# A 32-byte constant that shifts the weight ring of a one-core decoder layer by 32 bytes

## The chip, the core and the metric

The kernel runs on one core of one Trainium2 chip, in one launch. The metric is the time of the device in microseconds (us). Lower is better. Engine names are those of the profile: PE is TensorE (matmuls), PEld its weight loads, DVE is VectorE, ACT is ScalarE, POOL is GpSimd, SP is SyncE, which issues most of the DMAs.

## What is computed

One decoder layer on 512 tokens of width 1024, all in float32. Cut to its frame, the reference is:

```python
h = rms_norm(x, attn_norm[l])
proj = h @ w_in[l]
q_da, k_da, v_da, rw_cols, q_mem = jnp.split(proj, [c1, c2, c3, c4], axis=-1)
o_da = diff_attention(q_da, k_da, v_da, positions, ...)
o_rw = rwkv7_time_mix(rw_cols, ...)
mem_n = rms_norm(mem, mem_norm[l])
o_mem = memory_attention(q_mem, mem_n, w_mem_kv[l], ...)
x = x + jnp.concatenate([o_da, o_rw, o_mem], axis=-1) @ w_out[l]
xn = rms_norm(x, ffn_norm[l])
x = x + hierarchical_moe(xn, w_group_router[l], ..., w_e_gate[l], w_e_up[l], w_e_down[l])
```

The mixture has 16 experts of hidden width 512. Each token goes to two of them. Every expert has three weight matrices of 1024 x 512 numbers, so the expert weights alone are 16 x 3 x 2 MB.

## The kernel before

**The weights.** All weight matrices come through one stream (`WeightStream`, lines 72 to 118). A chunk is 128 partitions x 1024 float32 numbers (512 KB). It is loaded by SP (line 87) into a raw slot, and then split into a high and a low part: ACT rounds it to `whi` (line 96), and DVE subtracts (`wlo`, line 97). Both parts have the type float32r. Raw slots are the ring's `raw0` and `raw1`, later also buffers that are done with (`f`, `kT`, `qT`, `u`, `r_t`, `k_t`, `gg`), the `lraw`, `xhi` and `xlo` tiles of the pool `late`, and five `eraw` tiles of the pool `ex`. The parts sit in four pairs `whi0`/`wlo0` to `whi3`/`wlo3` of the ring, and for a while in two pairs `xhi`/`xlo`. At most 10 loads are in flight.

**The matmuls.** A product is three matmuls (`mm3`, lines 242 to 245): high by high, low by high, high by low. In the trace `pp<-whi,xh` means that `whi` is the moving operand, which streams through the array, and `xh` the stationary one, which the weight load puts there beforehand.

- RWKV columns (`cols_unit`, line 349): the weights are stationary and the normed input `hm_h`, `hm_l` moves, 512 columns a matmul.
- The other projections (`proj`, line 368) and the output projection (`out_part`, line 979): the weights move, 256 columns a matmul, and `hm_h`, `hm_l` (or, for the memory, `v_da`, `qT`) are stationary.
- Experts (lines 1264 to 1347): 96 gathered tokens are stationary (`xh`, `xl`, `hh`, `hl`), and the weights move, 512 columns a matmul. An expert has 48 matmuls for gate and up (`in_product`) and 24 for down (`down`), 8 transposes of the gathered tokens (line 1267) and 4 of the hidden values (line 1289).

**The order.** It is made when the program is built: a weave of generators with priorities, and then a scheduler that simulates the engines. Before the experts stand the projections, woven with the RWKV chain and the attention (to about 285 us), then the second half of the output projection and the routing (to about 342 us), then the experts.

**The places of the buffers.** Each pool takes a stretch of each partition's on-chip memory. On the left, from address 0 upward, lie `const`, `rc`, `wk`, `ring`, `bigr`, and then `biga`, whose place `late` takes over. On the right, up to the end, lie `hm`, later `rt`, then `ex`. Pools take space in steps of 32 bytes. The ring's tiles are 4096 bytes long and follow each other without a gap.

Of the kernel before, what the change touches and what calls it, by code (L numbers as in the profile page):

```python
# [10 lines left out]
F32 = mybir.dt.float32  # L11
# [9 lines left out]
P = 128  # L21
# [7 lines left out]
CAP = 96  # L29
# [40 lines left out]


class WeightStream:
    """Weight chunks in the order of their use: raw load, high part, low part, each in a ring of slots."""

    def __init__(self, tc):
        self.tc, self.nc, self.depth, self.flight = tc, tc.nc, DEPTH, []
# [42 lines left out]


class Weave:
    """Emits the steps of several streams in the order of their estimated times."""

    def __init__(self, tc):
        self.tc, self.live, self.now = tc, [], 0.0
# [25 lines left out]
def hybrid_layer_kernel(ctx, tc, x, mem, positions, cols, w_in, w_kv, w_out, wa2, g2, ffn, wr, br,  # L151
# [4 lines left out]
    const = ctx.enter_context(tc.tile_pool(name="const", bufs=1))  # L156
# [14 lines left out]
    def pp():  # L171
        return psp.tile([P, 512], F32, name="pp", bufs=4)

    def pc():
        return pools["ps"].tile([P, 512], F32, name="pc", bufs=2)

    def pt():
        return pools["ps"].tile([P, 512], F32, name="pt", bufs=2)

    ring = ctx.enter_context(tc.tile_pool(name="ring", bufs=1))  # L180
# [10 lines left out]
    def bR(name, shape, dtype=F32):  # L191
        return bigr.tile(shape, dtype, name=name)

    def b4(name, shape, dtype=F32):
        return biga.tile(shape, dtype, name=name)

# [1 line left out]
    A.preload_act_table_set("sigmoid_and_others")  # L198
    xs = [bR("f1", [P, 2, D]), bR("f2", [P, 2, D])]
    xt = [xs[t // 2][:, t % 2, :] for t in range(NT)]  # L200
# [82 lines left out]
        first = A.activation(hi, ps, AF.Copy, scale=g)  # L283
        return first, V.scalar_tensor_tensor(lo, ps, g, hi.bitcast(F32), op0=ALU.mult, op1=ALU.subtract)

# [1 line left out]
    banks = [pp() for _ in range(4)] + [pt() for _ in range(2)] + [pc() for _ in range(2)]  # L287
    held = [ws.pair.pop() for _ in range(3)]
    ws.pump()
# [35 lines left out]
        V.tensor_scalar(ext[:, E_DQ + h:E_DQ + h + 1], col[:, C_DQ:C_DQ + 1], -0.125 / SLOPES[h], None, op0=ALU.mult)  # L325
    V.tensor_scalar(ext[:, E_SUB:E_SUB + 1], col[:, C_SUB:C_SUB + 1], 1.0 - LAM_INIT, None, op0=ALU.mult)

# [1 line left out]
    r_t = bR("r_t", [P, 2, S])  # L329
    k_t = bR("k_t", [P, 2, S])  # L330
    v_t = b4("v_t", [P, 2, C + S])
# [144 lines left out]
        ws.cool()  # L476
        flags.add("proj")

# [1 line left out]
    lw = b4("prod", [P, 512])  # L480
    wa2_sb = lw[:, 0:256]
    g2_sb = lw[:, 256:512]
# [34 lines left out]
    def rwkv():  # L517
# [83 lines left out]
                V.tensor_mul(bk[sr(q), :, o::2, 64 - q * 64:128 - q * 64], part(k_t, q, o), part(ip, q, o))  # L601
            yield 2.4

# [1 line left out]
        for ci in range(4):  # L605
            for q in range(2):
                ps = pc()
# [56 lines left out]
            yield 1.5  # L664
        flags.add("bk_done")

# [1 line left out]
        V.memset(rs[:, 0:1024:33], 1.0)  # L668
        for s in range(30, -1, -1):
            n = 32 - s  # L670
# [87 lines left out]
        yield from inverse(0)  # L758
        wv.spawn(other(), RW_PRI, OTHER)

# [1 line left out]
        y_sb = bR("r_t", [P, NT, 256])  # L762
        V.memset(sav[sr(0), 0], 0.0)
        for c in range(NCH):
# [34 lines left out]
        flags.add("rwkv")  # L799
        ws.pump()  # L800

# [1 line left out]
    lp = const.tile([P, 2], F32, name="lp")  # L803
    lam = const.tile([P, 2], F32, name="lam")
    nlam = const.tile([P, 1], F32, name="nlam")
    offs = [0, 128, 384, 768]

    dist = b4("dist", [P, 1280])
# [166 lines left out]
            closes[k]()  # L975
        flags.add("att")

# [1 line left out]
    def out_part(ps, t, i, w, ks, k0, k1, lead=0):  # L979
        mix_hi, mix_lo = mix["hi"], mix["lo"]  # L980
        tk = slice(t * P, (t + 1) * P)
        for k in ks:
            hi, lo = w[k // 4]
            ah, al, o = mix_hi[:, k, tk], mix_lo[:, k, tk], ps[:, i * 256:(i + 1) * 256]
            T.matmul(o, ah, hi[:, k % 4, :], start=k == k0 and i == lead, stop=False, skip_group_check=True)  # L985
            T.matmul(o, ah, lo[:, k % 4, :], start=False, stop=False, skip_group_check=True)  # L986
            T.matmul(o, al, hi[:, k % 4, :], start=False, stop=k == k1, skip_group_check=True)  # L987
# [14 lines left out]
    wv.spawn(projections())  # L1002
    wv.spawn(norm_mem())
    wv.spawn(rwkv(), RW_PRI)
    wv.run()
    ba_ctx.close()
    psum_ctx.close()

# [1 line left out]
    late = ctx.enter_context(tc.tile_pool(name="late", bufs=1, reuse_waits="tile"))  # L1010
    ws.raw.extend(late.tile([P, 1024], F32, name=f"lraw{i}") for i in range(6))
    extra = [(late.tile([P, 1024], F32R, name=f"xhi{i}"), late.tile([P, 1024], F32R, name=f"xlo{i}")) for i in range(2)]
# [6 lines left out]
    def pl(n):  # L1019
        return pools["ps"].tile([P, 96], F32, name="pl", bufs=2)[:, 0:n]  # L1020
# [169 lines left out]
                for _ in range(t):  # L1190
                    T.matmul(warm[:, 0:128], onb, onb[:, 0:128], start=True, stop=True)

# [1 line left out]
    gslot = rc.tile([P, NE], F32, name="gslot")  # L1194
    gidx = rc.tile([P, NE], I32, name="gidx")
    sidx = rc.tile([P, NE], I32, name="sidx")
# [149 lines left out]
    down(*turn_h(sl, True), sidx[0:CAP, NE - 1:NE], gslot[0:CAP, NE - 1:NE], True)  # L1346
    ws.cool()

# [1 line left out]
    pk = pl(32)  # L1350
    for t in range(NT):
        T.matmul(pk[:, 0:NE], onb, member[:, t, :], start=t == 0, stop=t == NT - 1)
# [72 lines left out]
```

## Time and profile before

| | before |
|---|---|
| median of 3 runs | 636.5 us (636.15 to 637.94) |
| span of the profiled execution | 635.0 us |
| PE busy | 605.9 us, 95% |
| PEld busy | 486.2 us, 77% |
| DVE busy | 500.9 us, 79% |
| ACT busy | 413.0 us, 65% |
| DMA moved | 144.17 MB, mean 227 GB/s |

The span runs from the first to the last instruction of the profiled execution. Its own time beyond that is not given apart; the median of the runs lies 1.5 us above the span. PE's busy time counts a matmul until its modelled end, so matmuls that follow each other overlap in it: what a matmul costs is read from the distance of two starts, not from its duration.

### The profile page before, as it was taken

Reading aid. Unit: us, or ns where it says so; the run is one execution under the profiler, and the core shown is the slowest. Engines: PE = TensorE matmul, PEld = TensorE weight load, DVE = VectorE, ACT = ScalarE, POOL = GpSimd, SP = SyncE. Lnnn points to the kernel's source line nnn. Section 1 sums busy time; section 2 is a strip of 40 time slices with the busy share of each in tenths; the row PEclk is TensorE's granted clock in tenths of the full one; section 3 lists DMA queues with packets and bytes.
Section 4 is the critical chain, followed back from the end, with each engine's and each line's share of the span. In section 5 each row is a group of like instructions: output and inputs, shape, how many; then the busy total and the mean of one; then the engine's idle time right before and its main releaser. Section 6 shows DMA issues by size and latency. Waiting matters only on the chain.

```text
span 635.0 us, 10856 instructions
## 1 busy us (share of the span) xinstructions
PE 605.9 (95%) x3970; PEld 486.2 (77%) x3970; DVE 500.9 (79%) x893; ACT 413.0 (65%) x622; POOL 124.1 (20%) x129
## 2 busy tenths in 40 slices
PE   3899999999999998999999999999999999999992
PEld 3777899999998887769997677777776777777771
DVE  5754988699846698646468999999999999988991
ACT  3667433544457774655246778888888888888880
POOL 6701010344400123304001011110011111320001
PEclk9999999999999999999999999999999999999997
DMA  8523244222332033659698999999999999799913
GB/s 304 167 67 101 66 128 122 78 91 67 102 83 69 1 134 123 243 176 354 237 338 284 358 341 366 382 356 357 362 356 359 361 371 370 251 369 375 336 26 54
DMA packets 77501, 144.17 MB, mean 227 GB/s; under 512 B 12832, under 2 KB 30496, under 8 KB 77440
## 3 DMA queue, kind: packets, MB, share of 16 engines
q1 hardware_dynamic: 69200, 126.07, 56.1%
q0 software_dynamic: 3760, 13.24, 8.9%
q10 hardware_dynamic: 4480, 4.09, 2.0%
q8 instruction: 33, 0.54, 0.3%
q14 instruction: 28, 0.23, 0.1%
HBM read 131.72 MB, written 11.67 MB: 226 GB/s over the span
## 4 chain that ended last, share of the span: by engine, by line
PE 90%; DVE 4%; ACT 2%; DMA 2%; POOL 1%; issue 1%; POOLq 0%; ACTq 0%
PE pp L243 17%; PE pp L245 17%; PE pp L244 17%; PE py L244 4%; PE py L245 4%; PE py L243 4%; PE pp L985 3%; PE pp L986 2%; PE pp L987 2%; PE pp L1267 1%; PE pt L909 1%; PE pc L609 1%; PE py L1123 1%; PE pt L934 1%; PE pl L1090 1%; PE pp L1289 1%
## 5 line engine op out<-in xcount | busy, mean ns | idle before, releaser
L245 PE MATMUL pp<-whi,xl 128*96 128x512 f32 x264 | 104.0, 395 | 0.0
L244 PE MATMUL pp<-wlo,xh 128*96 128x512 f32 x264 | 103.8, 394 | 0.0
L243 PE MATMUL pp<-whi,xh 128*96 128x512 f32 x264 | 101.2, 394 | 0.8 <-ACT xh L1254 0.8
L97 DVE TENSOR_TENSOR wlo<-raw,whi 128x1024 fp32r<-128x1024 f32 x42 | 52.0, 1244 | 19.9 <-ACT whi L96 16.1
L1315 POOL DMA_INDIRECT out<-ye,sidx x16 | 23.2, 1452 | 226.1 <-DVE gidx L1217 105.8
L96 ACT ACTIVATE whi<-raw 128x1024 fp32r<-128x1024 f32 x42 | 44.1, 1058 | 33.0 <-PE pp L245 17.9
L243 PE MATMUL pp<-whi,hm_h 128*128 128x256 f32 x224 | 63.7, 285 | 0.0
L245 PE MATMUL pp<-whi,hm_l 128*128 128x256 f32 x224 | 62.8, 280 | 0.0
L244 PE MATMUL pp<-wlo,hm_h 128*128 128x256 f32 x224 | 62.7, 280 | 0.0
L243 PEld LDWEIGHTS pp<-whi,xh 128*96 128x96 f32 x264 | 42.5, 161 | 19.6 <-ACT xh L1254 1.3
L245 PEld LDWEIGHTS pp<-whi,xl 128*96 128x96 f32 x264 | 42.6, 161 | 18.4
L244 PEld LDWEIGHTS pp<-wlo,xh 128*96 128x96 f32 x264 | 42.5, 161 | 18.2
L244 PE MATMUL py<-wlo,hh 128*96 128x512 f32 x120 | 47.9, 399 | 0.0
L245 PE MATMUL py<-whi,hl 128*96 128x512 f32 x120 | 47.1, 392 | 0.0
L243 PE MATMUL py<-whi,hh 128*96 128x512 f32 x120 | 47.0, 392 | 0.0
L97 DVE TENSOR_TENSOR wlo<-u,whi 128x1024 fp32r<-128x1024 f32 x34 | 41.3, 1238 | 6.6 <-ACT whi L96 6.5
L97 DVE TENSOR_TENSOR wlo<-lraw,whi 128x1024 fp32r<-128x1024 f32 x36 | 42.6, 1217 | 2.8 <-ACT whi L96 2.7
L243 PEld LDWEIGHTS pp<-whi,hm_h 128*128 128x128 f32 x224 | 42.1, 188 | 1.5 <-issue 1.1
L244 PEld LDWEIGHTS pp<-wlo,hm_h 128*128 128x128 f32 x224 | 42.1, 188 | 0.9 <-issue 0.5
L245 PEld LDWEIGHTS pp<-whi,hm_l 128*128 128x128 f32 x224 | 42.1, 188 | 0.3
L96 ACT ACTIVATE whi<-lraw 128x1024 fp32r<-128x1024 f32 x36 | 37.1, 1058 | 5.1 <-PE pp L245 3.6
L96 ACT ACTIVATE whi<-u 128x1024 fp32r<-128x1024 f32 x34 | 35.1, 1055 | 4.6 <-PE pp L245 2.2
(397 smaller groups left out, 1555.3 us busy)
## 6 DMA issues: line engine op xcount, KB each, us to landing
raw<-in_w_in SPq DMA_DIRECT2D x22, 512.0 KB, 3.6
u<-in_wd SPq DMA_DIRECT2D x12, 512.0 KB, 8.0
lraw<-in_wg SPq DMA_DIRECT2D x12, 512.0 KB, 11.3
lraw<-in_wu SPq DMA_DIRECT2D x12, 512.0 KB, 8.7
lraw<-in_wd SPq DMA_DIRECT2D x12, 512.0 KB, 12.4
f<-in_wg SPq DMA_DIRECT2D x11, 512.0 KB, 7.2
u<-in_wu SPq DMA_DIRECT2D x11, 512.0 KB, 12.0
eraw<-in_wd SPq DMA_DIRECT2D x10, 512.0 KB, 13.5
```

The lines of the kernel that those rows point to most:

```text
L96: nc.scalar.activation(hi, slot, AF.Copy)
L97: nc.vector.tensor_sub(lo, slot, hi.bitcast(F32))
L243: T.matmul(ps, ah, bh, start=first, stop=False)
L244: T.matmul(ps, ah, bl, start=False, stop=False)
L245: T.matmul(ps, al, bh, start=False, stop=last)
L609: T.matmul(ps[:, h * P:(h + 1) * P], bk[sr(q), ci, h], u1[sr(q), q, ci, h], start=True, stop=True)
L909: T.matmul(po[:, 0:P], aws[i % 2][:, kb * P:(kb + 1) * P], qk["v"][:, kb, h * P:(h + 1) * P], start=kb == 0, stop=kb == qb)
L934: T.matmul(po[rows, :], mv[:, mb, h * 64:(h + 1) * 64], aws[mb][:, 0:512], start=mb == 0, stop=mb == 1)
L985: T.matmul(o, ah, hi[:, k % 4, :], start=k == k0 and i == lead, stop=False, skip_group_check=True)
L986: T.matmul(o, ah, lo[:, k % 4, :], start=False, stop=False, skip_group_check=True)
L987: T.matmul(o, al, hi[:, k % 4, :], start=False, stop=k == k1, skip_group_check=True)
L1315: G.indirect_dma_start(out, bass.IndirectOffsetOnAxis(ap=si, axis=0), ye, None, compute_op=ALU.add)
```

## The change

A tile `even` of 128 x 8 float32 numbers, 32 bytes a partition, is taken from the pool `const`. Nothing writes or reads it. Comments and two docstrings go as well, and the code is otherwise the same.

```diff
     lp = const.tile([P, 2], F32, name="lp")
     lam = const.tile([P, 2], F32, name="lam")
     nlam = const.tile([P, 1], F32, name="nlam")
+    const.tile([P, 8], F32, name="even")
     offs = [0, 128, 384, 768]
```

Everything that lies to the left and after `const` moves up by 32 bytes. Where the buffers begin in a partition, in bytes, with the rest after division by 64:

| buffers | before | after |
|---|---|---|
| `whi0`, and with it the whole ring, `raw` too | 15776 (32) | 15808 (0) |
| `f1`, and with it all of `bigr` (`f`, `kT`, `qT`, `u`, `r_t`, `k_t`, `gg`) | 52640 (32) | 52672 (0) |
| `v_da`, and with it the large tiles of `biga` | 122272 (32) | 122304 (0) |
| `lraw0`, and with it `lraw`, `xhi`, `xlo`, `xg` | 122272 (32) | 122304 (0) |
| `hm_h`, `hm_l` (right side) | 196576 (32) | unchanged |
| `xh`, `xl`, `hh`, `hl`, `ye`, `eraw` (right side) | 222720 (0) and so on, all 0 | unchanged |

By the rest after division by 256, the ring goes from 160 to 192, and `eraw` lies at 0 before and after.

The order of the instructions is the same on all five engines: the same 4168 rows on PE, 1034 on DVE, 682 on ACT, 156 on POOL and 386 on SP, with the same waits. The addresses are all that differs.

## Rows read from the trace of the kernel before

**Rows 1.** The page, section 1 (busy time) and section 4 (the chain).

```profile
PE 605.9 (95%) x3970; PEld 486.2 (77%) x3970; DVE 500.9 (79%) x893; ACT 413.0 (65%) x622; POOL 124.1 (20%) x129
...
PE 90%; DVE 4%; ACT 2%; DMA 2%; POOL 1%; issue 1%; POOLq 0%; ACTq 0%
```

**Rows 2.** Busy time in five stretches of the experts, each from transposes to transposes.

```profile
core 0: us, PE busy (x) PEld busy (x) DVE busy (x) ACT busy (x) POOL busy (x), PEclk, DMA share, GB/s
385.75:403.61 17.86, 17.86 (x91) 12.79 (x89) 16.99 (x26) 14.77 (x18) 2.43 (x2) 1.00 1.05 369
421.45:439.31 17.86, 17.86 (x91) 12.80 (x90) 16.99 (x26) 14.77 (x18) 2.43 (x2) 1.00 1.05 362
510.72:528.57 17.85, 17.85 (x90) 12.79 (x89) 16.98 (x26) 14.76 (x18) 2.43 (x2) 1.00 1.05 367
564.37:582.00 17.63, 17.63 (x87) 12.57 (x85) 15.97 (x18) 14.76 (x18) 1.46 (x1) 1.00 1.05 384
600.00:617.00 17.00, 17.00 (x78) 11.95 (x77) 15.40 (x16) 13.93 (x17) 1.42 (x1) 1.00 0.23 55
```

**Rows 3.** Timeline of PE in an expert: start us, duration us, what.

```profile
414.69 0.40 PE L244 MATMUL pp<-wlo,xh 128*96 128x512 f32 x1
414.93 0.39 PE L245 MATMUL pp<-whi,xl 128*96 128x512 f32 x1
415.16 0.39 PE L243 MATMUL pp<-whi,xh 128*96 128x512 f32 x1
...
417.45 0.39 PE L244 MATMUL py<-wlo,hh 128*96 128x512 f32 x1
417.68 0.39 PE L245 MATMUL py<-whi,hl 128*96 128x512 f32 x1
...
420.89 0.39 PE L243 MATMUL pp<-whi,xh 128*96 128x512 f32 x1
```

**Rows 4.** Timeline of PE in the projections: `hm` stationary, then `v_da`, `qT` stationary.

```profile
131.78 0.28 PE L244 MATMUL pp<-wlo,hm_h 128*128 128x256 f32 x1
131.89 0.28 PE L245 MATMUL pp<-whi,hm_l 128*128 128x256 f32 x1
...
133.59 0.28 PE L245 MATMUL pp<-whi,hm_l 128*128 128x256 f32 x1
...
75.85 0.28 PE L243 MATMUL pp<-whi,v_da 128*128 128x256 f32 x1
...
77.28 0.28 PE L243 MATMUL pp<-whi,v_da 128*128 128x256 f32 x1
```

**Rows 5.** The chain in order of time: two matmuls of plain float32, then transposes.

```profile
77.57 0.86 PE pc L594 x2
...
350.83 0.55 PE pp L1289 x4
...
385.91 0.66 PE pp L1267 x8
```

**Rows 6.** Groups of instructions by line: the matmuls with moving weights.

```profile
L243 PE MATMUL pp<-whi,xh 128*96 128x512 f32 x264 | 101.2, 394 | 0.8 <-ACT xh L1254 0.8
L243 PE MATMUL py<-whi,hh 128*96 128x512 f32 x120 | 47.0, 392 | 0.0
L243 PE MATMUL pp<-whi,hm_h 128*128 128x256 f32 x224 | 63.7, 285 | 0.0
L985 PE MATMUL pp<-whi,hm_h 128*128 128x256 f32 x96 | 25.4, 294 | 0.4 <-ACT pown L879 0.4
```

**Rows 7.** Groups of instructions by line: the two halves of the split, by raw slot.

```profile
L97 DVE TENSOR_TENSOR wlo<-lraw,whi 128x1024 fp32r<-128x1024 f32 x36 | 42.6, 1217 | 2.8 <-ACT whi L96 2.7
L97 DVE TENSOR_TENSOR wlo<-eraw,whi 128x1024 fp32r<-128x1024 f32 x25 | 29.4, 1219 | 2.4 <-ACT whi L96 2.4
L96 ACT ACTIVATE whi<-lraw 128x1024 fp32r<-128x1024 f32 x36 | 37.1, 1058 | 5.1 <-PE pp L245 3.6
```

**Rows 8.** Busy time in two stretches: loads into `f` to `kT`, then into `eraw`.

```profile
404.30:409.60 5.30, 5.30 (x28) 3.74 (x27) 4.60 (x11) 3.98 (x5) 1.90 (x2) 1.00 1.05 395
...
566.10:571.00 4.90, 4.90 (x23) 3.40 (x22) 3.48 (x5) 4.85 (x6) 1.46 (x1) 1.00 1.05 408
```

**Rows 9.** Timeline of SP and of ACT: the last load's issue, and the last split.

```profile
592.42 0.33 SPq L87 DMA_DIRECT2D f<-in_wd  x1
...
618.73 1.04 ACT L96 ACTIVATE whi<-f 128x1024 fp32r<-128x1024 f32 x1
```

**Rows 10.** Timeline of DVE in an expert: three splits back to back, and a wait.

```profile
408.09 1.23 DVE L97 TENSOR_TENSOR wlo<-lraw,whi 128x1024 fp32r<-128x1024 f32 x1 [0.70 <-ACT whi L96]
...
409.31 3.48 DVE L97 TENSOR_TENSOR wlo<-lraw,whi 128x1024 fp32r<-128x1024 f32 x3
412.71 2.44 DVE L97 TENSOR_TENSOR wlo<-raw,whi 128x1024 fp32r<-128x1024 f32 x2
```

## The prediction

> **What bounds the kernel.** I read the page first, then the experts stretch by stretch, then single matmuls. The page has PE busy for 95% of the span, and 90% of the chain that ended last runs over PE [rows 1]. The reader is to see that nothing else is near it as an average, and then to ask what PE itself is doing. The stretches of the experts answer that: PE is busy for the whole of each, and three experts far apart take 17.86, 17.86 and 17.85 us although the DMA rate differs between them [rows 2]. A time that repeats so well is PE's own pace, not a wait. So only what changes the distance between two matmuls is worth anything here.
>
> That distance is longer than the columns need. The granted clock is 1.00 in these stretches, the 2.4 GHz level, so 512 columns take 213.3 ns at one a cycle. From 414.69 to 420.89 us there are 28 matmul starts, so 27 distances in 6.20 us, 229.6 ns each [rows 3]. For a whole expert, 17.85 us less 12 transposes (0.66 and 0.55 us by their rows [rows 5]) leaves 16.64 us for 72 matmuls, 231 ns each, with four small ones in it. In the projections, 17 starts with 256 columns lie 16 distances or 1.81 us apart, 113.1 ns each, where the columns need 106.7 [rows 4]. The excess is thus 6.4 ns for 256 columns and 16 to 18 ns for 512. Now 6.4 ns is the time of 15 to 16 columns, and 16 columns of four bytes are 64 bytes. Two plain float32 matmuls of 512 columns, whose moving operand also starts 32 bytes past a multiple of 64, take 0.86 us, 430 ns each [rows 5]. That is twice 213.3 and only 3.4 ns more: where a column lasts two cycles, there is nearly no excess. So the excess belongs to streams that need four bytes every cycle.
>
> **The change part by part.**
>
> *The unused tile.* No instruction is added, moved or removed, and no wait. Its own cost is nothing. All that can count is the new address.
>
> *Splits on ACT and DVE.* The old trace has both alignments side by side. DVE takes 1217 ns from `lraw` (32 past 64) and 1219 ns from `eraw` (at 64) [rows 7]. I cost reading at nothing. Writing `whi` and `wlo` to an aligned place is not in the trace; ACT's 1058 ns for 1024 elements bounds a gain, and PE, which is late for nothing that ACT makes, hides it [rows 2].
>
> *Loads.* These have both alignments too. Over 404.3 to 409.6 us the loads go to slots at 32 past 64 and the core moves 395 GB/s; over 566.1 to 571.0 us they go to `eraw` and it moves 408 [rows 8]. That is 3% by rates which also hold gathers and scatters. I count it as zero on the path, since the last load is issued at 592.42 us, DMA is nearly idle over 600 to 617, and the last split starts at 618.73 [rows 2, 9]. The cover is some 15 us of loads done ahead; without it each of the 12 loads of an expert would have to be paid for.
> The Trainium skill has a rule that speaks against a gain here (DMA: Bandwidth & Descriptors, How a descriptor splits into AXI transactions): a transfer that does not start at a multiple of 256 bytes pays an extra transaction. By it `eraw`, at such a multiple, says nothing on slots that go from 160 to 192. The sum by it is the same, as the loads are covered.
>
> *Matmuls with moving weights in the experts.* There are 264 x 3 and 120 x 3, 1152 in all [rows 6]. The trace of before has no float32r stream that starts at a multiple of 64, so the price is bounded: at most the whole excess of 18 ns goes (20.7 us in all), at least nothing, and a loss is not excluded (a rival below). I take the value nearest to a row with the same columns at no hurry. A run of 1024 bytes that starts 32 past a multiple of 64 touches 17 pieces of 64 bytes and not 16, and 16 columns are 6.7 ns; for 512 columns that is 13.3 ns. Plain float32 keeps 1.7 ns per 512 columns over its cycles [rows 5], so I take 11.6 ns. The rest of the excess, 3 to 5 ns, I put down to the weight load that runs beside and leave it. 1152 x 11.6 ns = 13.4 us, or 0.84 us an expert.
>
> *Matmuls with moving weights before the experts.* 224 x 3 and 96 x 3 by the large groups [rows 6], and about 64 x 3 in smaller ones, 1152 in all. At 6.4 ns less half of 1.7, so 5.5 ns, that is 6.3 us. I count half, 3.2 us, because these are woven with the RWKV chain and the attention, whose small steps wait for each other. The ends are 0 and 7.4 us. Where `hm` moves, nothing changes, as it stays where it was.
>
> *What is late next.* An expert would take 17.85 - 0.84 = 17.01 us. DVE has one wait of 0.70 us in an expert and otherwise works back to back, three splits in 3.40 us by their starts [rows 10]; it could not go below some 17.0 us. So DVE is next, and it stops any further gain in the experts. The loads need 13.4 us of their 15 us lead. Both just hold.
>
> *The sum.* Span 635.0 - 13.4 - 3.2 = 618.4 us. The median of the runs shown lies 1.5 us above the span, so the time is 619.9, told as 620 us.
>
> **The rivals.**
>
> *The excess has nothing to do with the start.* It could be a limit of the read itself: 512 columns in 227 to 231 ns are 9 bytes a nanosecond in each partition. Nothing in the trace of before tells this from the forecast, as all float32r streams start 32 past 64. For it: the excess grows with the columns (6.4, then 13 and more) as a rate would have it. Against it: it fits one more piece of 64 bytes per 1024 so exactly. Then all intervals stay, the faster loads are covered, and the time is 636.5 us.
> The Trainium skill would have it so (SBUF — State Buffer, in the section on door 1): it tells of lines of 16 bytes, and a start at 32 is a multiple of 16 already. No run here shows lines of 16 bytes.
>
> *The weight load beside the stream decides, and the new distance is worse.* The same matmul of 256 columns takes 113.1 ns with `hm` stationary, but 1.43 us for 12 distances, 119.2 ns, with `v_da` and `qT` [rows 4]. The moving weights lie 64 bytes apart from `hm` modulo 128, and 0 from `v_da` and `qT`. So the two streams may meet in the same part of the memory, by their distance. The change moves the weights by 32 bytes and leaves `hm`, `xh` and `hh` where they are: `hm` comes to 32, the experts' tokens to 64. If at 32 the projections cost what they cost at 0, then (224 + 96 + 32) x 3 = 1056 matmuls lose 6.1 ns, 6.4 us, and the time is 643 us. It decides from 1.8 ns a matmul on (1.9 us). Against it: the experts are at 32 apart now, and their excess over 13.3 is 3 to 5 ns with 96 columns to load, so I would expect half of that price, 640 us.
>
> *The same, to the good.* The experts come to a distance of 64, at which the projections have no more than their 6.4 ns. If that takes 3 to 5 ns off 1152 matmuls, it is 3.5 to 5.8 us, less half of 6.4 us lost in the projections: 634 us.
>
> **How the numbers follow.** A measurement of this kernel can tell about 0.3% from no change, 1.9 us. I give the forecast 0.45, the read limit 0.27, the loss by the weight load 0.20 and the gain by it 0.08. Faster: 0.45 + 0.07 = 0.52. Slower: 0.20. Same: 0.28, the read limit and the smallest of the others. The forecast's own range is 613 to 630: at the low end the whole excess goes before the experts (7.4 us) and these gain 16 x 1.0 us, a little beyond DVE's bound as I read it; at the high end 6 ns go from each of the experts' matmuls and nothing before them. The range to hold 8 in 10 has to take in the read limit and most of the loss: 613 to 641.
>
> **What would show it.** In the trace of after, experts far apart should repeat at 17.0 us, not 17.85; starts of 512 columns at about 218 ns and of 256 columns at about 108. If they stand at 230 and 113, the read limit is right. If 256 columns with `hm` stationary go to 116 or more while the experts do not gain, it is the weight load. If matmul distances shrink and the experts do not, look for PE waiting on `wlo` (DVE late) or ACT waiting on a load (the lead used up). The loads into `lraw` should then run at the rate of those into `eraw`, or not, if only multiples of 256 count. The forecast is wrong if the experts keep their 17.85 us.

## The result: 0.8% slower

The kernel with the change takes 641.61 us (median of 4 runs, 640.61 to 643.53), the kernel before 636.33 us on the same chip (median of 4, 634.97 to 637.94). The ratio is 1.0079, with a 95% interval of 1.0060 to 1.0098. That is slower by more than the 0.3% that a measurement of this kernel can tell, and 0.6 us beyond the upper end of the range. The forecast was 620 us; the rival "the weight load beside the stream decides, and the new distance is worse" gave 640 to 643 us.

**The profile after.** The profiled execution took 643.53 us, 1.9 us above its median, with a span of 641.8 us against 635.0. The page, sections 1 and 4:

```profile
PE 612.2 (95%) x3970; PEld 491.1 (77%) x3970; DVE 506.4 (79%) x893; ACT 413.5 (64%) x622; POOL 127.3 (20%) x129
...
PE 89%; DVE 4%; ACT 2%; DMA 2%; POOL 1%; issue 1%; POOLq 0%; ACTq 0%
```

PE still bounds everything, with the same instructions; it is 6.3 us busier [rows 1]. The stretches that answer to those of before [rows 2, 8], the first four each an expert from transposes to transposes, the last two loads into old buffers and into `eraw` (us, busy us of PE, PEld, DVE, ACT and POOL with counts, granted clock, DMA share, GB/s):

```profile
391.83:409.71 17.88, 17.88 (x90) 12.79 (x89) 16.98 (x26) 14.77 (x18) 2.43 (x2) 1.00 1.05 369
427.60:445.49 17.89, 17.89 (x91) 12.81 (x90) 16.99 (x26) 14.78 (x18) 2.42 (x2) 1.00 1.04 361
517.03:534.92 17.89, 17.89 (x91) 12.80 (x89) 16.99 (x26) 14.78 (x18) 2.43 (x2) 1.00 1.05 366
570.80:588.49 17.69, 17.69 (x87) 12.59 (x85) 15.98 (x17) 14.79 (x18) 1.46 (x1) 1.00 1.05 384
...
410.40:415.70 5.30, 5.30 (x29) 3.76 (x28) 4.56 (x10) 3.98 (x5) 1.91 (x2) 1.00 1.06 399
572.60:577.50 4.90, 4.90 (x23) 3.39 (x22) 3.42 (x5) 4.89 (x6) 1.46 (x1) 1.00 1.06 409
```

An expert still repeats to 0.01 us, at 17.88 to 17.89 us instead of 17.85. It should have come to 17.0. The clock is the same 1.00. Now single matmuls: the timeline of PE after, the same instructions as in [rows 4, 3], namely 17 starts in the projections with `hm` stationary, 13 with `v_da` and `qT`, and 28 in an expert:

```profile
133.89 0.28 PE L244 MATMUL pp<-wlo,hm_h 128*128 128x256 f32 x1
134.01 0.28 PE L245 MATMUL pp<-whi,hm_l 128*128 128x256 f32 x1
...
135.79 0.28 PE L245 MATMUL pp<-whi,hm_l 128*128 128x256 f32 x1
...
77.09 0.28 PE L243 MATMUL pp<-whi,v_da 128*128 128x256 f32 x1
...
78.52 0.28 PE L243 MATMUL pp<-whi,v_da 128*128 128x256 f32 x1
...
420.77 0.40 PE L244 MATMUL pp<-wlo,xh 128*96 128x512 f32 x1
...
427.04 0.39 PE L243 MATMUL pp<-whi,xh 128*96 128x512 f32 x1
```

From here on an interval is the time between two starts, and a distance is one of places in memory. The 16 intervals with `hm` take 1.90 us instead of 1.81, or 118.3 ns each by the unrounded starts instead of 113.4. The 12 with `v_da` and `qT`, where both operands moved by 32 bytes, take 1.43 us as before. The 27 in the expert take 6.27 us instead of 6.20. So none of these three became faster. The one that became clearly slower, `hm` stationary, is one in which only the weights moved.

Where the time accrues is read from the start of the same instruction in both traces. For `v_da` [rows 4] it is 1.24 us later (77.09 against 75.85), for the pair with `hm` 2.11 us (133.89 against 131.78), for the first transposes of an expert [rows 2] 6.08 us (391.83 against 385.75), and the last split, which stood at 618.73 [rows 9], is 6.63 us later. The timeline of ACT after, the last split:

```profile
625.36 1.04 ACT L96 ACTIVATE whi<-f 128x1024 fp32r<-128x1024 f32 x1
```

So 4.8 of the 6.6 us come between 76 and 386 us, in the projections and the output projection, and 0.5 us in the experts. The first 76 us give 1.2 us. Of that 0.5 us is there by 20 us already; the profiled executions of e3 and e12 below stand 0.8 us earlier and 0.4 us later at 80 us with their paces unchanged up to there, so I put nothing on half a microsecond. The other 0.7 us is that of the RWKV columns, in the table below.

All pairs of neighbours say which kinds pay. I paired every matmul start with the next, where both belong to the same shape and nothing lies between, and gave each pair the distance of the two operands' places: start of the stationary one less start of the moving one, modulo 256.

| pairs (count) | distance, before to after | mean ns, before | mean ns, after | sum |
|---|---|---|---|---|
| weights move, 256 columns, `hm` stationary (953) | 64 to 32 | 114.2 | 118.3 | +3.9 us |
| weights move, 256 columns, `v_da`, `qT` stationary (88) | 0, 0 | 119.5 | 119.3 | 0.0 us |
| `hm` moves, 512 columns, weights stationary (175) | 192 to 224 | 229.2 | 233.2 | +0.7 us |
| experts, 512 columns (545) | 224 to 192 | 230.2 | 232.4 | +1.2 us |
| experts, 512 columns (563) | 96 to 64 | 231.9 | 230.9 | -0.6 us |

(Pairs over 130 or 245 ns are left out of the counts and the means, as a wait lies in them.) The sum is 5.2 us; the two medians differ by 5.3, the two profiled spans by 6.8. In this table only pairs whose distance changed have another pace: `v_da` and `qT` moved together with the weights, and theirs stayed.

### The profile page after: what moved, and what is told of

Its sections match the earlier page's. It is cut to its first block, busy times and chain, and to the rows that moved or that the text cites. A ratio compares the mean times of both kernels' runs of the same rounds, so it can differ in the third digit from the quotient of the medians.

```text
span 641.8 us, 10856 instructions
## 1 busy us (share of the span) xinstructions
PE 612.2 (95%) x3970; PEld 491.1 (77%) x3970; DVE 506.4 (79%) x893; ACT 413.5 (64%) x622; POOL 127.3 (20%) x129
## 4 chain that ended last, share of the span: by engine, by line
PE 89%; DVE 4%; ACT 2%; DMA 2%; POOL 1%; issue 1%; POOLq 0%; ACTq 0%
PE pp L243 17%; PE pp L244 16%; PE pp L245 16%; PE py L244 4%; PE py L243 4%; PE py L245 4%; PE pp L986 3%; PE pp L987 2%; PE pp L988 2%; PE pt L910 2%; PE pp L1268 1%; DVE wlo L97 1%; PE pc L609 1%; PE py L1124 1%; PE pt L935 1%; PE pl L1091 1%
## 5 line engine op out<-in xcount | busy, mean ns | idle before, releaser
L97 DVE TENSOR_TENSOR wlo<-lraw,whi 128x1024 fp32r<-128x1024 f32 x36 | 42.6, 1218 | 2.8 <-ACT whi L96 2.5
```

The source lines that it names most:

```text
L97: nc.vector.tensor_sub(lo, slot, hi.bitcast(F32))
```

## The experiments

The theory at this point: what counts is the distance between the place of the moving operand and that of the stationary one. Rivals: the new start of the weights; the new places of raw slots and work buffers; a limit that knows no addresses, with the loss coming from elsewhere.

### e1: move `hm` instead of the ring

```diff
     h_lo = hm.tile([P, KC, S], F32R, name="hm_l")
+    hm.tile([P, 8], F32, name="hpad")
```

In the kernel before. `hm` lies on the right side, so it moves down by 32 bytes; the ring and all on the left stay.

> The kernel before, with the unused 32 bytes on the other side: hm_h and hm_l move down by 32 bytes, the ring and all behind it stay where they were (32 past a multiple of 64). Theory (distance): what counts is how far the stationary operand lies from the moving one, 64 bytes before, 32 with the change; here it is 32 too, so 256 columns with hm stationary take 117 to 118 ns again instead of 113, 512 moving columns of hm 234 instead of 229, the experts keep their 17.85 us, and the time is 641 to 642 us. Rival (start): moving weights that start at a multiple of 64 are slower by themselves; here they don't, so 113 ns and 636.3 us.

Measured: 640.68 us (6 runs) against 636.97, ratio 1.0064 (1.0049 to 1.0079). The timeline of PE, the same 17 starts:

```profile
133.42 0.28 PE L244 MATMUL pp<-wlo,hm_h 128*128 128x256 f32 x1
...
135.31 0.28 PE L245 MATMUL pp<-whi,hm_l 128*128 128x256 f32 x1
```

These are 1.89 us, 118 ns each, as after the change, though the weights start at 32 past a multiple of 64 as before. `hm` moving with 512 columns rose to 233.1 ns, and the experts kept 17.853 us. So it is the distance that costs, and neither the weights' own start nor the other buffers are needed for it. The loss here is 3.7 us of the change's 5.3, a little under the 641 to 642 us expected; of the rest, 0.6 us is the experts' own in the table above.

### e2: the change, and `hm` 96 bytes down

```diff
     h_lo = hm.tile([P, KC, S], F32R, name="hm_l")
+    hm.tile([P, 24], F32, name="hpad")
```

In the changed kernel. This makes the distance 64 modulo 128 again, as the prediction had counted it, and 192 modulo 256.

> The change, with hm_h and hm_l moved down by 96 bytes, so that they lie 64 bytes from the weights again modulo 128. Theory (distance): 256 columns with hm stationary take 113 ns again; the experts keep the 17.89 us of the change; 636.5 to 637.5 us. Rival (start): the weights still start at a multiple of 64, so 117 to 118 ns and 641.6 us. If the distance counts modulo 256 rather than 128, neither of the two need hold, as it goes from 64 to 192.

Measured: 641.83 us (6 runs), ratio 1.0070 (1.0051 to 1.0090). The 17 starts take 117.8 ns each, and the experts 17.887 us as under the change. So 192 is not as good as 64, and the prediction's count modulo 128 falls.

### e3: everything behind the ring, without the ring

```diff
     ba_ctx = ExitStack()
     biga = ba_ctx.enter_context(tc.tile_pool(name="biga", bufs=1))
+    bigr.tile([P, 8], F32, name="even")
```

In the kernel before: raw slots behind the ring, work buffers and late buffers move up by 32 bytes to multiples of 64, the ring and `hm` stay.

> Half of the change: the unused 32 bytes behind the ring, so the ring stays where it was, and the raw slots and work buffers behind it (f, kT, qT, u, lraw, xhi, v_da and so on) begin at multiples of 64. Theory (distance): hm and the experts see the same ring as before, so 113 ns, 17.85 us and 636.3 us; only the memory's projections change, as v_da and qT come to 32 from the weights: 117 to 118 ns instead of 120, some 0.2 us. Rival (loads or work buffers): the loss comes from slots at multiples of 64, and the time is up to 641.6 us.

Measured: 637.25 us (12 runs), ratio 1.0008 (0.9997 to 1.0019). The same 17 starts take 113.3 ns each. Work buffers and load slots at multiples of 64 bring nothing, and cost nothing that the runs can tell. The 91 pairs that take their weights from `xhi` and `xlo`, which did move, rose from a median of 113 to 117 ns, 0.4 us. Another 0.5 us has no change of distance behind it: of the pairs of `hm` with the ring, which both stayed, 67% run at 115 ns or less, in the kernel before 81% (means 114.9 and 114.2 ns). The 17 starts lie in a stretch that kept its pace.

### e4: sixteen distances, two starts, two widths of the load

```diff
+    def sweep(ncol, n, m):
+        for s in range(16):
+            o = s * 8 + m
...
+                    T.matmul(swept[0][0:ncol, 0:n], wa[:, o:o + ncol], wb[:, m:m + n], start=True, stop=True)
...
+    sweep(96, 512, 0)
+    sweep(96, 512, 8)
+    sweep(32, 512, 0)
+    sweep(32, 512, 8)
```

At the end of the kernel before, for 256 columns against 128 stationary ones too: eight matmuls at each of 16 distances in steps of 32 bytes. With `m` 0 the moving operand starts 32 past a multiple of 64, with `m` 8 at one.

> The kernel before, with 768 matmuls after the last expert whose results nothing uses: weights stationary against other weights moving, 8 each at 16 distances from 0 to 480 bytes in steps of 32, with 128 stationary and 256 moving columns, 96 and 512, 32 and 512, each with the moving start 32 past and at a multiple of 64. Theory (distance): the interval depends on the distance and not on the start; at 0 about 120 ns, at 32 about 117, at 64 about 113 for 256 columns, and it repeats every 128 bytes or a multiple of it. Rival (start): the two halves of each set differ at every distance. With 32 stationary columns the weight load is a third as long or less, so if the excess over the columns comes from the load, 512 columns go down towards 215 ns; if it is a limit of the moving read, they stay at 227. The time is some 120 us above before's.

Measured: 775.21 us in one run. The timeline of PE: five blocks of the first series, and the first start of each of the other five:

```profile
629.14 1.07 PE L1359 MATMUL pp<-whi,whi 128*128 128x256 f32 x8
630.05 1.09 PE L1357 MATMUL pp<-whi,whi 128*128 128x256 f32 x8
630.98 0.40 PE L1359 MATMUL pp<-whi,whi 128*128 128x256 f32 x2
...
632.88 1.11 PE L1359 MATMUL pp<-whi,whi 128*128 128x256 f32 x8
633.83 0.28 PE L1357 MATMUL pp<-whi,whi 128*128 128x256 f32 x1
...
638.57 0.41 PE L1359 MATMUL pp<-whi,whi 128*128 128x256 f32 x2
...
653.75 0.39 PE L1359 MATMUL pp<-whi,whi 128*96 128x512 f32 x1
...
683.35 0.39 PE L1359 MATMUL pp<-whi,whi 128*96 128x512 f32 x1
...
712.96 0.40 PE L1359 MATMUL pp<-whi,whi 128*32 128x512 f32 x1
...
742.54 0.40 PE L1359 MATMUL pp<-whi,whi 128*32 128x512 f32 x1
```

A series has 128 matmuls. With 96 stationary columns it takes 29.60 us from the start at 32 past 64 (653.75 to 683.35), and 29.61 us from a multiple of 64 (683.35 to 712.96): 231.3 ns each in both. With 256 columns the second half of the series at 32 past 64 (630.98 to 638.57) and the whole of the other (638.57 to 653.75) run at 118.6 ns each; waits lie in the first half. This refutes the prediction's step on the start by itself. With 32 stationary columns a series takes 29.58 us (712.96 to 742.54). So with 512 columns a load of a third of the columns leaves the excess, and it is not the length of the weight load that makes it there. For 256 columns the width was not tried. There it could count, as the groups of PEld in the changed kernel show (experts, then `hm` stationary; the last numbers are busy us, ns of one, idle us before):

```profile
L243 PEld LDWEIGHTS pp<-whi,xh 128*96 128x96 f32 x264 | 42.6, 161 | 19.4 <-ACT xh L1255 1.3
L245 PEld LDWEIGHTS pp<-whi,hm_l 128*128 128x128 f32 x224 | 42.2, 188 | 0.3
```

Between the experts' loads PEld has idle time, between those for 256 columns next to none.

In the series with 256 columns the block at 629.14, at distance 192, takes 0.91 us for eight, 114 ns each; later blocks at the same distance took 117 to 119 ns. So one distance can show either pace. At distance 64, where about 113 ns was expected, all three blocks without a wait run at 118 ns (the first of them is 632.88 to 633.83). That expectation failed: the sweep, in which eight matmuls in a row have the same two operands, does not single out 64.

### e5, e6, e7, e9, e10, e11: the map of the distances

In the kernel before, the unused constant at the place of the change, with 16, 32, 64, 56, 48 or 40 numbers instead of 8:

```diff
     nlam = const.tile([P, 1], F32, name="nlam")
+    const.tile([P, 16], F32, name="even")
```

> The unused constant is 64 bytes a partition instead of 32: ring, work buffers and late slots move up by 64 and so begin again 32 past a multiple of 64, like before; the matmuls of hm_h stand at distance 0 to their stationary operand, those of the experts at 32 and 160 (mod 256). Theory of the relative address: what counts is the distance, and 0 is not the good one (v_da with qT, both moved, stood at distance 0 in the kernel before and took 120 ns); 256 columns against hm at 117 to 120 ns instead of 113, 1.0 to 1.3% slower than before at most, about 640 to 643 us. Rival, the start within 64 bytes decides: same start as before, so 113 ns and 636.5 us.

> The unused constant is 128 bytes: distance 192 for hm with 256 moving columns (the distance of the run that moved hm by 96 under the change), experts at 224 and 96, the two values of before with their places exchanged. Relative address with a period of 256 bytes: hm 118 ns, 640 to 641.5 us, expert period 17.85 us as before. Relative address with a period of 128 bytes (already weakened): 113 ns, 636.5 us. Start within 64 bytes: 636.5 us.

> The unused constant is 256 bytes: every distance is what it was before, modulo 256, though every address of the ring, the work buffers and the late slots has moved. Relative address with a period of 256: 113 ns against hm, 636.0 to 637.5 us, no difference. Rival, a longer period or the absolute address (a bank of SBUF, the neighbour's slot): 640 us or more, or some other number.

> The unused constant is 224 bytes: distance 96 (mod 256) for 256 columns against hm, 0 and 128 in the experts. What is open is which distances allow the short interval, 113 ns: measured so far 0 (120), 32 (117), 64 (113), 192 (118). Only one distance is good: 117 to 120 ns, 640 to 643 us. The good distances are a band around 64, or the stream is slow where the weights begin less than 64 bytes behind the moving rows: 113 ns or less, 636.5 us or less.

> The unused constant is 192 bytes: distance 128 for 256 columns against hm, half a period from the worst one (0, 120 ns); 160 and 32 in the experts, where the two runs with these values showed a period of 17.85 us. Only 64 is good: 117 to 120 ns, 640 to 643 us. The interval grows with the nearness of the distance to 0: 113 ns or less, 636.5 us or less.

> The unused constant is 160 bytes: distance 160 for 256 columns against hm, between 128 and 192 (118 ns); 64 and 192 in the experts as under the change, so a period of 17.89 to 17.90 us there and 0.5 us more over the experts. Only 64 is good: 117 to 120 ns, 640.5 to 643.5 us. A second good place opposite to the bad ones: 113 ns, 637 us.

The timeline of PE in e5, the same 17 starts at distance 0:

```profile
132.51 0.28 PE L244 MATMUL pp<-wlo,hm_h 128*128 128x256 f32 x1
...
134.43 0.28 PE L245 MATMUL pp<-whi,hm_l 128*128 128x256 f32 x1
```

And in e7, where all is 256 bytes further on, the distance is 64 again:

```profile
131.73 0.28 PE L244 MATMUL pp<-wlo,hm_h 128*128 128x256 f32 x1
...
133.55 0.28 PE L245 MATMUL pp<-whi,hm_l 128*128 128x256 f32 x1
```

That is 1.92 and 1.82 us. All variants with these 17 starts, by distance (the experts' distances are those of the 545 and the 563 pairs):

| run | ring up | distance to `hm` | ns each, 16 intervals | experts' distances | period of an expert, us | ratio (95% interval) |
|---|---|---|---|---|---|---|
| e5 | 64 | 0 | 120.0 | 160, 32 | 17.853 | 1.0077 (1.0055 to 1.0099) |
| change | 32 | 32 | 118.3 | 192, 64 | 17.887 | 1.0079 (1.0060 to 1.0098) |
| before | 0 | 64 | 113.4 | 224, 96 | 17.853 | |
| e7 | 256 | 64 | 113.3 | 224, 96 | 17.853 | 1.0001 (0.9988 to 1.0015) |
| e9 | 224 | 96 | 117.4 | 0, 128 | 17.867 | 1.0075 (1.0051 to 1.0099) |
| e10 | 192 | 128 | 118.6 | 32, 160 | 17.833 | 1.0056 (1.0036 to 1.0076) |
| e11 | 160 | 160 | 120.1 | 64, 192 | 17.913 | 1.0084 (1.0065 to 1.0103) |
| e6 | 128 | 192 | 117.7 | 96, 224 | 17.900 | 1.0050 (1.0033 to 1.0066) |

The period is 256 bytes: e7 moved the ring by eight times the change's step and lost nothing. In this kernel, of the seven distances tried (224 was not), 64 alone is good; the kernel before stood on it. The means over all pairs with `hm` stationary that hold no wait agree: 114.2 ns at 64 (before and e7), 117.1 to 119.8 ns at the others. Three of these variants (the change, e9, e11) start the weights at multiples of 64, and none gained. In the experts the distance is worth at most 0.08 us an expert (17.833 to 17.913), 1.3 us over 16.

### e8: move the experts' buffers alone

```diff
+    ex_p.tile([P, 16], F32, name="epad")
     full = nc.values_load(mosti[0:1, 0:1], min_val=0, max_val=S)
```

In the kernel before: only the expert pool moves, down by 64 bytes.

> The kernel before with 64 unused bytes at the end of the expert pool: only the expert buffers xh, xl, hh, hl, sl, ye and the raw slots eraw move down by 64, so the experts' distances become 32 and 160; ring and hm stay. Relative address: the stream before the experts is as before (113 ns against hm); in the experts, where 512 columns run at 231 ns, the sweep had its shortest mean near distance 32 (229 ns against 230 to 233): 0 to 2 ns on 1,152 matmuls, so 634.5 to 637.5 us. If the distance costs nothing in the experts: expert period 17.85 us, 636.5 us.

Measured: 636.72 us (12 runs), ratio 0.9997 (0.9983 to 1.0011), 17.853 us an expert, 113.3 ns at the 17 starts. One group of the experts' pairs gained 1.2 ns (231.9 to 230.7) and the other lost 1.1 (230.2 to 231.3). There is nothing to win in the experts by distance that these runs can tell, and little to lose: 0.6 of the change's 5.2 us in the table of pairs.

### e12: the rule on other operands

```diff
     ba_ctx = ExitStack()
     biga = ba_ctx.enter_context(tc.tile_pool(name="biga", bufs=1))
+    bigr.tile([P, 16], F32, name="even")
```

In the kernel before, like e3 with 64 bytes.

> Cross-check of the rule on other operands: 64 unused bytes between the ring and the buffers behind it, so the ring and hm stay and everything between them moves up by 64. The 91 matmuls whose stationary operand is v_da or qT come to distance 64 from the moving weights of the ring (0 before, where they took 120 ns; 32 in the run with 32 bytes, 118 ns); the 91 matmuls that read their weights from the slots xhi, xlo with hm stationary come from 64 to 0 (113 ns at 64). If 64 is good for every pair of this shape: the first group falls to 113 ns, the second rises to 120 ns, the 900 others stay at 113; the two cancel within 1 us, 635.5 to 638 us. If the good distance belongs to hm alone: v_da and qT stay at 117 to 120 ns.

Measured: 637.47 us (10 runs), ratio 1.0011 (0.9998 to 1.0024). The 91 pairs with weights from `xhi` and `xlo` rose from 113 to a median of 120 ns at distance 0, as expected. The 91 with `v_da` and `qT` came to 64 and did not settle at 113: 19 of them are below 115 ns and the median is 118. The timeline of PE, the 13 starts of [rows 4]:

```profile
76.27 0.28 PE L244 MATMUL pp<-whi,v_da 128*128 128x256 f32 x1
...
77.68 0.28 PE L244 MATMUL pp<-whi,v_da 128*128 128x256 f32 x1
```

1.41 us instead of 1.43. So 64 allows the short pace and does not ensure it. Even with `hm` at 64, in the kernel before, 18% of the 953 pairs stand above 115 ns.

Those come in whole stretches. The timeline of PE before, the ends of a short and of a long one, with nothing else on PE in between:

```profile
135.43 0.28 PE L244 MATMUL pp<-wlo,hm_h 128*128 128x256 f32 x1
...
146.76 0.28 PE L245 MATMUL pp<-whi,hm_l 128*128 128x256 f32 x1
...
303.47 0.28 PE L986 MATMUL pp<-wlo,hm_h 128*128 128x256 f32 x1
...
306.07 0.28 PE L987 MATMUL pp<-whi,hm_l 128*128 128x256 f32 x1
```

The first has 100 intervals in 11.33 us, 113 ns each, the second 22 in 2.60 us, 118 ns each. I take all stretches of nine or more such intervals without a wait or other work of PE. From the fifth interval on each keeps one pace, 26 the short one and 6 the long one. In e7 and e8, which keep this distance, the same six are long. Where the buffers behind the ring moved (e3, e12), other stretches are long too, although neither the ring nor `hm` moved.

## Why the prediction was wrong

**What bounds the kernel: right.** PE's pace decides, and only the time between two matmul starts matters. Such intervals make up the result: 5.2 us by the pairs, 5.3 by the medians.

**The step that failed: "the excess belongs to streams that need four bytes every cycle", put down to the start, 17 pieces of 64 bytes instead of 16.** From this came 13.4 us in the experts and 3.2 us before them. The runs show in its place: a float32r stream of 512 columns takes 231.3 ns at either start (e4), and the experts at multiples of 64 take 17.89 us. The agreement of 6.4 ns with 16 columns was a coincidence of sizes. All float32r streams of the trace started 32 past 64, as the prediction itself said; a number that fits, where the other case isn't in the trace, is no evidence for the cause. It deserved less than 0.45. The row that stood beside it was misread, too: line 594 runs twice in the kernel and has four records in the trace, so the two records of 0.43 us in [rows 5] are one plain float32 matmul, not two. A column still lasts two cycles in each record, so the sum does not hang on it.

**The read limit** is right for the base: no distance and no start brought 256 columns below 113 ns on a stretch. The Trainium skill (SBUF — State Buffer, in the section on door 1) tells of lines of 16 bytes, by which a start at 32 is no worse than one at 64. By that no start would have gained anything, and e4 agrees with it at this point, 29.60 against 29.61 us. That rival's time, 636.5 us, is wrong, as it knew no distances.

**The rival of the weight load was right in its place, its sign and its size.** It counted 1056 matmuls at up to 6.1 ns, and 640 to 643 us. Measured are 4.1 ns on 953 pairs, 3.9 us, and 0.7 and 0.6 us in two kinds of pairs that it did not count. Its mark (256 columns with `hm` at 116 or more while the experts do not gain) is what the trace shows. Two of its steps were off or open: it counted the distance modulo 128, which e2 refutes, and its name says more than is shown. The pace goes by the relative place of the two operands; that two reads meet there is an argument, and the part of the load's length was tested only with 512 columns, where it made no difference (e4). Its chance of 0.20 was too low: the two paces of [rows 4] were the only rows shown in which something about addresses went with a difference, and they spoke for this rival.

**The same rule to the good** gave the experts 3 to 5 ns at distance 64. Modulo 256 they came to 64 and 192; one group gained 1.0 ns and the other lost 2.2.

**Splits and loads: right.** DVE's split from `lraw` takes 1218 ns, against 1217 [rows 7], now that both the slot and the destination start at multiples of 64. It is the page's group after:

```profile
L97 DVE TENSOR_TENSOR wlo<-lraw,whi 128x1024 fp32r<-128x1024 f32 x36 | 42.6, 1218 | 2.8 <-ACT whi L96 2.5
```

Loads into slots that now start at multiples of 64 run at 399 GB/s against 395 [rows 8], those into `eraw` at 409 against 408. A start at a multiple of 64 did not close the gap. The Trainium skill (DMA: Bandwidth & Descriptors, How a descriptor splits into AXI transactions) lets only multiples of 256 count, and the trace agrees so far as rates of two stretches can. Nothing of it reached the path. The bound by DVE at 17.0 us an expert was never met.

**The range** ended at 641, because it took in "most of the loss". It left out the rival's upper end of 643, and the result fell 0.6 us outside. With 0.20 on a case, cutting its upper half was too tight.

## What to carry to other kernels

Moving a buffer moves every distance between it and what it is used with. Before aligning something, list the pairs of operands that are read together, and look in the trace whether the same instruction already runs at two paces with different partners; that row says more than a size that happens to fit. An unused tile of 32 bytes is a cheap probe, and worth trying at several sizes: here five other sizes at the same place lost 0.5 to 0.8% as well, 256 bytes changed nothing, and none beat the kernel before.

## What was not expected

- A stream of 256 float32r columns against 128 stationary ones has two lasting paces at a distance of 64 modulo 256, 113 to 114 and 117 to 119 ns. The short one was most of the stream only there. At 192 it shows in 10 to 14% of the pairs (e2, e6), and at 0, 32, 96, 128 and 160, with `hm` stationary, in 2% or less.
- The pace belongs to a stretch and not to a pair, as the lines under e12 show. So something at the start of a stretch counts besides the distance, and the runs do not show what.
- The shortest pace is still 6 to 7 ns above the columns' own 106.7 ns for 256 columns. Neither a start at a multiple of 64, nor any distance tried, nor, with 512 columns, a load a third as wide removed the excess. Its cause stays open, and so does why 64 is the good distance.
- With 512 columns the order of the distances is another one: `hm` moving has its best mean at 0 (227.7 ns, e5) and stands at 229.2 at 192 and at 232 to 234 elsewhere.
